# Scaling and transposing the rows of x by f32 matmuls with diagonal matrices instead of DMA transposes, with eight row buffers and one recurrence moved to VectorE

## The chip, the cores and the metric

One core of a Trainium2 chip runs the whole program. The metric is device time in microseconds (us), lower is better. The time before is the median of 3 runs.

## What is computed

Two blocks run one after the other on x, 2048 rows of 1024 values, all f32. Only the first part of the first block is touched:

```python
def first_block(x, norm_gain, w_in, ssm_a_re, ssm_a_im, ssm_log_dt, ...):
    h = rmsnorm(x, norm_gain) @ w_in          # 1024 -> 3072 columns
    # 512 columns u for the state-space mixer, 512 z, and 4 x 512 for a gated short convolution
    y_ssm = s5_mixer(u, a_re, a_im, log_dt, b_re, b_im, c_re, c_im, d, ...)
    y_conv = short_conv_mixer(...)
    # gates, w_out, residual, norm
```

`rmsnorm` divides each row by its root mean square and multiplies by the gain. `s5_mixer` makes its discrete parameters from `a_re`, `a_im` and `log_dt` (exponentials, sines, cosines, a division) and runs a complex linear recurrence along the rows. The second block (adaptive layer norm, a convolution module, a gated recurrence, chunked attention, a feed-forward part) is far larger, and no line of it is edited.

## The kernel before

TensorE (PE) works on f16. Each f32 operand is split into a high f16 part and a low f16 part that holds the rest, and each product is made of three f16 matmuls: high by low, low by high, high by high, the lines L417, L418 and L419 of the helper `mm3`. An activation split is made by `k.split`: the high part by ScalarE (ACT, L405), the low part by VectorE (DVE, L406). A scheduler (the Tile framework) fixes the order of the instructions on each engine at build time, from the order in which the program issues them and from the buffers they need. On the chip, each engine takes its own list strictly in order and waits where an operand is late.

`stage_in` is the stage that is edited. x is read in 16 tiles of 128 rows, into a ring of `NX` buffers. For each tile, `x1(t)` sums the squares of the rows (ACT, L410) and makes the reciprocal root by some ten very small DVE operations (L387 to L396). `x2(t)` then splits the scaled rows into hi and lo, and two DMA transposes, issued on the SP queue (L813, L814), put them into `xT`, four pairs of tiles with the 1024 columns on the partitions and 512 rows each. The rows in `xT` feed every product of the stage:

- `first(n)`, for n = 0 to 3, is done while the first four tiles and the first four weight blocks come in. It multiplies what has just become possible, in pieces of 128 rows: 24, 72, 120 and 168 matmuls, 384 in all. `first(n)` takes weight block n with the tiles before n, then tile n with the weight blocks 0 to n.
- `uproj(1)`, `uproj(2)` and `uproj(3)` do the other three groups of 512 rows: 96 matmuls of 512 columns each. `put_u` (ACT, L821) brings each result from PSUM into `u`.
- Then follow the other 20 weight blocks of w_in over all of `xT`, the long stream of 512-column matmuls that starts at 151 us in the profile. The text calls it the chunk stream.

The state-space parameters are a background task, `ssm_all`. From `t == 8` on the scheduler mixes its instructions into the loop. `ssm_params` reads `a_re`, `a_im` and `log_dt` (L473, L474, and L476 twice) and works on 128x16 values with more than 150 DVE operations, the first of which on `log_dt` is L445. `ssm_fb` then makes, for each of four groups `fb`, powers E and H by complex multiplications `cmul`, 48 tensor operations each, all on GpSimd (POOL, through `k.gtt`, L360); ACT copies H into wide tiles (L647, L648), and PE transposes E and multiplies (L628, L629, L637, L638).

The DMA that matters below reads one value per pair of groups and repeats it over 64 partitions:

```python
for g in range(2):
    nc.sync.dma_start(ldt[g * 64:(g + 1) * 64], a["ssm_log_dt"][0].rearrange("(r g) -> g r", g=2)[g].partition_broadcast(64))
```

Of the kernel before, what the change touches and what calls it, by code (L numbers as in the profile page):

```python
# [9 lines left out]
F32 = mybir.dt.float32  # L10
F16 = mybir.dt.float16
BF16 = mybir.dt.bfloat16
# [3 lines left out]
ALU = mybir.AluOpType  # L16
# [4 lines left out]
P = 128  # L21
T = 2048
D = 1024
KB = 8
# [2 lines left out]
RN = 1.5 * 2.0 ** 23  # L27
TWO_PI = 2.0 * math.pi
ALPHA = 2.0 ** 0.25
NX = 5  # L30


class Arena:
# [64 lines left out]
    def new(self, shape, dt=F32, name="t"):  # L98
        size = {F32: 4, I32: 4, F16: 2, BF16: 2, U8: 1}[dt]
        m = 1  # L100
        for d in shape[1:]:
            m *= d
        st, n = self.take(-(-m * size // 4))
        v = self.ap[:shape[0], st:st + n]
        if dt != F32:
            v = v.bitcast(dt)
        v = v[:, :m]
        if len(shape) > 2:
            names = ["d%d" % i for i in range(len(shape) - 1)]
            v = v.rearrange("p (%s) -> p %s" % (" ".join(names), " ".join(names)), **{nm: d for nm, d in zip(names[1:], shape[2:])})  # L110
        self.live[id(v)] = (v, st, n, name)
        return v
# [441 lines left out]
def ssm_fb(k, a, pm, fb, u_d, y_d):  # L554
    nc = k.nc
    gp = nc.gpsimd
    v = nc.vector
    NP = 4
    prs = slice(fb * 4, fb * 4 + 4)
    shp = [P, NP, 16]  # L560
    flat = lambda t: t.rearrange("p a b -> p (a b)")
    bc = lambda nm: pm[nm][:, prs].unsqueeze(2).to_broadcast(shp)
    new = lambda s, nm: k.new(s, F32, nm)
# [14 lines left out]
    Hr, Hi = new([P, NP, 8, 16], "Hr"), new([P, NP, 8, 16], "Hi")  # L578
    t1, t2 = new(shp, "cm1"), new(shp, "cm2")

    def cmul(orr, oi, xr, xi, yr, yi):
        k.gtt(t1, xi, yi, ALU.mult)
        k.gtt(orr, xr, yr, ALU.mult)
        k.gtt(orr, orr, t1, ALU.subtract)
        k.gtt(t2, xi, yr, ALU.mult)
        k.gtt(oi, xr, yi, ALU.mult)
        k.gtt(oi, oi, t2, ALU.add)

    cmul(Er[:, :, 0], Ei[:, :, 0], br, bi, bc("qr"), bc("qi"))
    k.free(br, bi)  # L590
    for j in range(7):
        cmul(Er[:, :, j + 1], Ei[:, :, j + 1], Er[:, :, j], Ei[:, :, j], bc("abr"), bc("abi"))
        if j == 3:
            yield
    yield
    C = []
    Cb = []
    for nm, c2 in zip(("ssm_c_re", "ssm_c_im"), cs2):
# [3 lines left out]
        pv = pt[:, :P].rearrange("p (r g h) -> p r g h", g=2, h=16)  # L602
# [4 lines left out]
        for g in range(2):  # L607
            sl = slice(g * 64, g * 64 + 64)
            nc.scalar.copy(c[sl], pv[sl, :, g])
            nc.scalar.mul(cb[sl, :, g], pv[sl, :, g], sgn)  # L610
        k.unbank(pt)
        C.append(c)
        Cb.append(cb)
    yield
    cmul(Hr[:, :, 0], Hi[:, :, 0], C[0], C[1], bc("abr"), bc("abi"))
    k.free(*C)
    for j in range(7):
        cmul(Hr[:, :, j + 1], Hi[:, :, j + 1], Hr[:, :, j], Hi[:, :, j], bc("abr"), bc("abi"))
        if j == 3:
            yield  # L620
    k.free(t1, t2)
# [23 lines left out]
    for g in range(2):  # L645
        sl = slice(g * 64, g * 64 + 64)
# [31 lines left out]
    for r in range(NP):  # L678
# [21 lines left out]
        t1, t2 = new([P, 256], "t1"), new([P, 256], "t2")  # L700
# [80 lines left out]
def stage_in(k, a, dr):  # L781
    nc = k.nc
    v = nc.vector
    gp = nc.gpsimd
    win = a["w_in"][0]
    inv_x = k.hold()
    gp.memset(inv_x, 1.0 / XS)
    xT = [k.pair([P, KB, TB], "xT%d" % tb) for tb in range(NTB)]
    gain = k.hold(KB)
    wu = Loader([Weight(k, win[:, f * P:(f + 1) * P], inv_x, rowmul=gain, mul=v.tensor_tensor if f < 3 else None) for f in range(4)])  # L790
    xs = {}

    ring = [k.new([P, D], F32, "x") for _ in range(NX)]

    def x0(t, after=None):
        xs[t] = ring[t % NX]
        if after is not None:
            v.tensor_copy(xs[t][:, 0:1], after)
        nc.sync.dma_start(xs[t], a["x"][0, t * P:(t + 1) * P, :])

    def x1(t):
        x = xs[t]
        hi, lo = k.pair([P, D], "xs")
        ss = k.sumsq(lo.bitcast(BF16), x)
        xs[t] = (x, hi, lo, k.rsqrt(ss, 1.0 / (D * XS * XS), 1e-6 / (XS * XS)))

    def x2(t):
        x, hi, lo, rs = xs.pop(t)
        k.split(hi, lo, x, rs)
        if t >= 16 - NX:  # L810
            k.free(x)
        sl = slice((t % 4) * P, (t % 4 + 1) * P)
        nc.sync.dma_start_transpose(out=xT[t // 4][0][:, :, sl], in_=hi)  # L813
        nc.sync.dma_start_transpose(out=xT[t // 4][1][:, :, sl], in_=lo)  # L814
        k.free(hi, lo)
        return lo[:, 0:1]

    u = [k.new([P, 8, 256], F32, "u") for _ in range(4)]

    def put_u(tb, fb, w, ps):  # L820
        nc.scalar.activation(u[fb][:, :, tb * 64:(tb + 1) * 64], ps.rearrange("p (c t) -> p t c", t=8), AF.Identity, scale=w.inv)  # L821
        k.unbank(ps)

    def uproj(tb):
        for fb in range(4):
            w = wu.get(fb)
            put_u(tb, fb, w, k.fm(w, xT[tb]))
            if tb == NTB - 1:
                w.free()
                nc.sync.dma_start(dr["u"][fb * P:(fb + 1) * P], u[fb])  # L830
                k.free(u[fb])
            k.bg.tick()

    def first(n):
        for t, f in [(t, n) for t in range(n)] + [(n, f) for f in range(n + 1)]:
            w = wu.ws[f]
            sl = slice(t * P, (t + 1) * P)
            k.mm3(ps0[f][:, sl], [(w.hi[:, kb], w.lo[:, kb]) for kb in range(KB)], [(xT[0][0][:, kb, sl], xT[0][1][:, kb, sl]) for kb in range(KB)])
        if n == 3:
            for f in range(4):  # L840
                put_u(0, f, wu.ws[f], ps0[f])

    x0(0)
    wu.ws[0].load()
    nc.sync.dma_start(gain, a["norm_gain"][0].rearrange("(k p) -> p k", p=P))
    for t in range(1, 4):
        x0(t)
    ps0 = [k.bank() for _ in range(4)]
    ssm = None
    for t in range(17):  # L850
        if 1 <= t <= 4:
            wu.ws[t - 1].split()
            x2(t - 1)
        if t == 4:
            for j in range(4, 8):
                x0(j)
        if t < 16:
            x1(t)
        if t < 4:
            if t:  # L860
                wu.ws[t].load()
            wu.ws[t].stat()
        if t > 4:
            x2(t - 1)
        if 1 <= t <= 4:
            first(t - 1)
        if t == 4:
            wu.n = [4, 4, 4]
        if 4 < t < 13:
            x0(t + 3)  # L870
        if t == 8:
            ssm = k.bg.add(ssm_all(k, a, dr), 1.0)
        if t == 10:
            uproj(1)
    uproj(2)
    uproj(3)
    cw = k.new([P, 4, 3], F32, "cw")
    for j in range(3):
        nc.sync.dma_start(cw[:, :, j], a["conv_w"][0, j].rearrange("(f p) -> p f", p=P))
    mod = k.bg.add(mod_rows(k, a, dr["mod"]), 0.8)  # L880
    cols = [c + fb * P for fb in range(4) for c in (2048, 1024, 1536, 2560)] + [512 + f * P for f in range(4)]
    chunks = Loader([Weight(k, win[:, c:c + P], inv_x, rowmul=gain) for c in cols])
    at = 0
    ssm[1] = SSM_RATE
    for fb in range(4):
        vv = k.new([P, 2 + T], F32, "vv")
        acc = k.new([P, T], F32, "acc")
        gp.memset(vv[:, 0:2], 0.0)
        for st in range(4):
            w = chunks.get(fb * 4 + st, 1)  # L890
            for tb in range(NTB):
                ps = k.fm(w, xT[tb])
                sl = vv[:, 2 + tb * TB:2 + (tb + 1) * TB]
                asl = acc[:, tb * TB:(tb + 1) * TB]
                if st == 0:
                    nc.scalar.activation(sl, ps, AF.Identity, scale=w.inv)
                elif st == 1:
                    v.scalar_tensor_tensor(sl, ps, w.inv, sl, op0=ALU.mult, op1=ALU.mult)
                    for j in range(3):
                        src = vv[:, j + tb * TB:j + (tb + 1) * TB]  # L900
                        if j == 0:
                            v.tensor_scalar(asl, src, cw[:, fb, 0:1], None, op0=ALU.mult)
                        else:
                            v.scalar_tensor_tensor(asl, src, cw[:, fb, j:j + 1], asl, op0=ALU.mult, op1=ALU.add)
                elif st == 2:
                    v.scalar_tensor_tensor(asl, ps, w.inv, asl, op0=ALU.mult, op1=ALU.mult)
                else:
                    zt = k.new([P, TB], F32, "zt")
                    nc.scalar.activation(zt, ps, AF.Silu, scale=w.inv)
                    v.tensor_tensor(asl, asl, zt, ALU.mult)  # L910
                    k.free(zt)
                k.unbank(ps)
                k.bg.tick()
            w.free()
            if st == 1:
                k.free(vv)
        nc.sync.dma_start(dr["yv"][fb * P:(fb + 1) * P], acc)
        k.free(acc)
    k.free(cw)
    return xT, chunks, ssm, mod  # L920
# [1349 lines left out]
XS = 1024.0  # L2270
# [84 lines left out]
```

## Time and profile before

| what | value |
|---|---|
| runs | 3268.93, 3275.31, 3273.25 us, median 3273.25 |
| profiled execution | 3276.22 us, span 3274.5, mean granted TensorE clock 0.967 |
| busy share | PE 93%, DVE 63%, ACT 34%, POOL 23% |
| first 151.5 us (stage up to the chunk stream) | PE busy 99.3 us (26.4 + 34.2 + 38.7 in three pieces) |
| the other 3123 us | PE busy 2948.9 us |

A row of the timeline reads: start, duration, engine, line, operation, output<-input, shape, and in brackets how long the engine had been idle before it and what ended that. Rows of a queue (SPq) are the issue of a DMA, not its transfer. Since PE is busy for nearly all of the later program, the first 151 us hold a good part of PE's idle time: 52 of 226 us.

### The profile page before, as it was taken

How to read it: one execution, taken by the hardware profiler on the slowest of the kernel's cores; microseconds unless marked ns; L12 is line 12 of the kernel's file. 1: busy time of each engine (PE TensorE's matmuls, PEld its weight loads, DVE VectorE, ACT ScalarE, POOL GpSimd, SP SyncE). 2: the span in 40 equal slices, each digit the busy share in tenths (PEclk: the TensorE clock that was granted, in tenths of full speed). 3: DMA queues.
4: the chain of work that ended last, by engine and by line, in shares of the span. 5: the costliest groups of instructions: out<-in, count | busy, mean ns of one | idle time of the engine just before them, and what ended most of it. 6: DMA issues, size and time to landing. Idle time of an engine off the chain costs nothing. (4 is left out here: it accounts for less than half of the span.)

```text
span 3274.5 us, 43302 instructions
## 1 busy us (share of the span) xinstructions
PE 3048.2 (93%) x16198; PEld 1532.2 (47%) x16198; DVE 2061.5 (63%) x4895; ACT 1116.8 (34%) x1745; POOL 760.0 (23%) x801
## 2 busy tenths in 40 slices
PE   6799999979799988999999878999999999899998
PEld 4344454534345654555555433444444444344443
DVE  5577887355864469999568877555555555543322
ACT  5322222584524565221333333444443333300000
POOL 0432533023332332110120223111111121023321
PEclk9899999989899998999999989999999999999999
DMA  8734443535773754100125798222331113723220
GB/s 181 166 92 111 121 125 80 120 100 152 215 219 74 138 117 106 39 14 33 62 78 140 170 250 216 90 78 78 102 110 54 58 52 119 244 68 113 68 73 31
DMA packets 549651, 364.57 MB, mean 111 GB/s; under 512 B 290152, under 2 KB 503592, under 8 KB 545344
## 3 DMA queue, kind: packets, MB, share of 16 engines
q1 hardware_dynamic: 549440, 361.81, 41.1%
q8 instruction: 127, 2.08, 0.3%
q14 instruction: 84, 0.69, 0.1%
HBM read 216.73 MB, written 84.70 MB: 92 GB/s over the span
## 5 line engine op out<-in xcount | busy, mean ns | idle before, releaser
L417 PE MATMUL psum<-arena 128*128 128x512 f16 (+2 forms) x4272 | 1601.9, 377 | 78.6 <-DMA arena<-arena 34.4
L418 PE MATMUL psum<-arena 128*128 128x512 f16 (+2 forms) x4272 | 1602.1, 376 | 8.2 <-DMA arena<-h_d 4.2
L419 PE MATMUL psum<-arena 128*128 128x512 f16 (+2 forms) x4272 | 1598.6, 376 | 0.2 <-DVE arena L406 0.2
L360 POOL TENSOR_TENSOR arena<-arena 128x64 f32<-128x64 f32 (+5 forms) x681 | 681.8, 1025 | 2089.2 <-DVE arena L2179 336.9
L417 PEld LDWEIGHTS <-arena 128*128 128x128 f16 x4272 | 426.0, 100 | 593.1 <-issue 101.1
L418 PEld LDWEIGHTS <-arena 128*128 128x128 f16 x4272 | 424.1, 99 | 492.1 <-issue 44.3
L419 PEld LDWEIGHTS <-arena 128*128 128x128 f16 x4272 | 424.2, 99 | 488.4 <-issue 26.1
L410 ACT ACTIVATE arena<-arena 128x1024 bf16<-128x1024 f32 (+2 forms) x218 | 237.7, 1091 | 487.0 <-DVE arena L2062 153.3
L406 DVE SCALAR_TENSOR_TENSOR arena<-arena,kept 128x1024 f16<-128x1024 f32 (+2 forms) x152 | 230.4, 1538 | 130.0 <-ACT arena L405 110.4
L2005 DVE TENSOR_TENSOR arena<-arena,psum 128x512 f32<-128x512 f32 x264 | 177.8, 684 | 206.0 <-PE psum L419 150.9
L405 ACT ACTIVATE arena<-arena,kept 128x1024 f16<-128x1024 f32 (+2 forms) x152 | 174.5, 1175 | 183.0 <-DVE kept L355 62.7
L406 DVE SCALAR_TENSOR_TENSOR arena<-arena,ring 128x1024 f16<-128x1024 f32 (+1 forms) x164 | 209.7, 1302 | 42.0 <-ACT arena L405 36.2
L405 ACT ACTIVATE arena<-arena,ring 128x1024 f16<-128x1024 f32 (+1 forms) x164 | 172.2, 1082 | 168.6 <-DVE ring L355 100.4
L1369 DVE SCALAR_TENSOR_TENSOR arena<-arena 128x512 f32<-128x512 f32 x240 | 177.9, 778 | 0.3
L1551 PE MATMUL psum<-arena 128*127 128x64 f32 (+6 forms) x896 | 106.2, 264 | 22.2 <-DVE arena L1554 21.1
L1551 PEld LDWEIGHTS psum<-arena 128*127 128x127 f32 (+6 forms) x896 | 102.0, 182 | 48.4 <-DVE arena L1554 29.8
L2179 DVE SCALAR_TENSOR_TENSOR arena<-psum,kept,arena 128x512 f32<-128x512 f32 x32 | 23.3, 747 | 144.0 <-PE psum L419 144.0
L770 DVE SCALAR_TENSOR_TENSOR arena<-arena 128x128 f32<-128x128 f32 x336 | 111.6, 367 | 1.8
L2051 ACT ACTIVATE arena<-arena,kept 128x1024 f32<-128x1024 f32 x44 | 49.8, 1142 | 124.1 <-DVE arena L2005 124.1
L1289 ACT ACTIVATE arena<-arena,ring,kept 128x640 f32<-128x640 f32 (+4 forms) x64 | 54.5, 851 | 81.8 <-DVE ring L1287 73.0
L373 PE MATMUL psum<-kept,ones 128*128 128x1 bf16 x82 | 13.3, 169 | 70.4 <-DVE kept L365 49.5
L1553 DVE TENSOR_TENSOR arena<-arena 128x256 f32<-128x256 f32 x112 | 54.9, 490 | 37.4 <-PE psum L1551 35.8
(318 smaller groups left out, 2583.2 us busy)
## 6 DMA issues: line engine op xcount, KB each, us to landing
arena<-in_w_in_dram SPq DMA_DIRECT2D x50, 512.0 KB
arena<-in_w_ada_dram SPq DMA_DIRECT2D x48, 512.0 KB
arena<-in_w_ffn_in_dram SPq DMA_DIRECT2D x44, 512.0 KB
arena<-in_w_ffn_out_dram SPq DMA_DIRECT2D x44, 512.0 KB
a_d<-arena SPq DMA_DIRECT2D x88, 256.0 KB
arena<-a_d SPq DMA_DIRECT2D x40, 512.0 KB
arena<-in_x_dram SPq DMA_DIRECT2D x32, 512.0 KB
x_d<-arena SPq DMA_DIRECT2D x32, 512.0 KB
```

What stands on the lines that cost most here:

```text
L360: self.nc.gpsimd.tensor_tensor(out, x, y, op)
L405: self.nc.scalar.activation(hi, src, AF.Identity, scale=s)
L406: self.nc.vector.scalar_tensor_tensor(lo, src, s, hi, op0=ALU.mult, op1=ALU.subtract)
L410: self.nc.scalar.activation(junk, src, AF.Square, accum_out=ss)
L417: self.nc.tensor.matmul(ps, lh, rh, start=start and i == 0, stop=False)
L418: self.nc.tensor.matmul(ps, lh, rl, start=False, stop=False)
L419: self.nc.tensor.matmul(ps, ll, rh, start=False, stop=stop and i == n - 1)
L770: v.scalar_tensor_tensor(ac, raw[:, kb], cc[:, kb:kb + 1], ac, op0=ALU.mult, op1=ALU.add)
L1369: v.scalar_tensor_tensor(acc[:, f], src, w, acc[:, f], op0=ALU.mult, op1=ALU.add)
L1551: nc.tensor.matmul(pv[:rows, bsl], KS[:, c * P:c * P + rows], q4[:, bsl], start=True, stop=True)
L1553: v.tensor_tensor(q4, q4, Fv[:, :, 0:1].to_broadcast([P, nb, hb]), ALU.mult)
L2005: v.tensor_tensor(out, x, ps, op)
```

## The change

- `NX` goes from 5 to 8, and the loads of x are issued in another place: the load of tile t + 3 in round t, from round 1 on.
- `x1` no longer makes room for hi and lo; it makes `dg`, the 128x128 identity times the reciprocal root of each row (DVE, L812).
- `x2` multiplies: for each of the 8 blocks of 128 columns, one f32 matmul with the block of x as the stationary operand and `dg` as the moving one (L819). That gives the block transposed and scaled, in two PSUM banks. ACT copies the banks into the hi half of `xT` (L826, 128x1024 from PSUM), and DVE subtracts hi from PSUM into the lo half (L827). The two DMA transposes go.
- The `ssm_all` task starts at `t == 7`, `uproj(1)` stands at `t == 9`, `uproj(2)` at `t == 13`.
- The H products of group `fb == 0` are made on DVE (L582 to L587).

```diff
-NX = 5
+NX = 8
...
     def x1(t):
         x = xs[t]
-        hi, lo = k.pair([P, D], "xs")
-        ss = k.sumsq(lo.bitcast(BF16), x)
-        xs[t] = (x, hi, lo, k.rsqrt(ss, 1.0 / (D * XS * XS), 1e-6 / (XS * XS)))
+        junk = k.new([P, D], BF16, "junk")
+        ss = k.sumsq(junk, x)
+        k.free(junk)
+        dg = k.new([P, P], F32, "dg")
+        v.tensor_scalar(dg, k.ident, k.rsqrt(ss, 1.0 / (D * XS * XS), 1e-6 / (XS * XS)), None, op0=ALU.mult)
+        xs[t] = (x, dg)
 
     def x2(t):
-        x, hi, lo, rs = xs.pop(t)
-        k.split(hi, lo, x, rs)
+        x, dg = xs.pop(t)
+        ps = k.bank(2)
+        for kb in range(KB):
+            nc.tensor.matmul(ps[:, kb * P:(kb + 1) * P], x[:, kb * P:(kb + 1) * P], dg, start=True, stop=True)
         if t >= 16 - NX:
             k.free(x)
+        k.free(dg)
+        pv = ps.rearrange("p (k t) -> p k t", t=P)
         sl = slice((t % 4) * P, (t % 4 + 1) * P)
-        nc.sync.dma_start_transpose(out=xT[t // 4][0][:, :, sl], in_=hi)
-        nc.sync.dma_start_transpose(out=xT[t // 4][1][:, :, sl], in_=lo)
-        k.free(hi, lo)
-        return lo[:, 0:1]
+        hi, lo = (xT[t // 4][x_][:, :, sl] for x_ in range(2))
+        nc.scalar.copy(hi, pv)
+        v.tensor_tensor(lo, pv, hi, ALU.subtract)
+        k.unbank(ps)
...
-        if 4 < t < 13:
+        if 0 < t < 13:
             x0(t + 3)
-        if t == 8:
+        if t == 7:
             ssm = k.bg.add(ssm_all(k, a, dr), 1.0)
-        if t == 10:
-            uproj(1)
-    uproj(2)
+        if t in (9, 13):
+            uproj(t // 4 - 1)
     uproj(3)
...
+    ht = v.tensor_tensor if fb == 0 else k.gtt
...
-    cmul(Hr[:, :, 0], Hi[:, :, 0], C[0], C[1], bc("abr"), bc("abi"))
+    cmul(Hr[:, :, 0], Hi[:, :, 0], C[0], C[1], bc("abr"), bc("abi"), ht)
```

The edit also moves instructions. Three places matter for what follows; the rows give the line, the operation, output<-input and the shape, and xN stands for N in a row.

The SP queue before, where the state-space parameters are issued; L799 loads a tile of x (here tiles 12 and 13), L813 and L814 are the transposes of earlier tiles:

```order
L799 DMA arena<-in_x_dram 128x1024
L813 DMA_TRANSPOSE arena<-arena 128x8x128
L814 DMA_TRANSPOSE arena<-arena 128x8x128
L799 DMA arena<-in_x_dram 128x1024
L474 DMA arena<-in_ssm_a_im_dram 128x16x1
L476 DMA arena<-in_ssm_log_dt_dram 64x16x1 x2
```

The SP queue after, from its beginning; L804 loads a tile of x, L169 a weight block:

```order
L804 DMA arena<-in_x_dram 128x1024
L169 DMA arena<-in_w_in_dram 128x8x128
L857 DMA kept<-in_norm_gain_dram 128x8x1
L804 DMA arena<-in_x_dram 128x1024 x3
L169 DMA arena<-in_w_in_dram 128x8x128
L804 DMA arena<-in_x_dram 128x1024
L169 DMA arena<-in_w_in_dram 128x8x128
L804 DMA arena<-in_x_dram 128x1024
L169 DMA arena<-in_w_in_dram 128x8x128
L804 DMA arena<-in_x_dram 128x1024 x4
L473 DMA arena<-in_ssm_a_re_dram 128x16x1
L474 DMA arena<-in_ssm_a_im_dram 128x16x1
```

The two loads of `log_dt` stand right behind these rows. They have moved ahead of the loads of x from tile 10 on, and nothing but the loads of tiles 0 to 9, four weight blocks, the gain, `a_re` and `a_im` is issued before them.

VectorE (DVE) before, around L445, the first operation that needs `log_dt`; L406 makes the lo half of a row tile, L538 to L540 work on `a_re` and `a_im`, L387 to L396 are the reciprocal roots:

```order
L406 SCALAR_TENSOR_TENSOR arena<-arena,ring 128x1024
L396 SCALAR_TENSOR_TENSOR ring<-ring 128x1
L392 SCALAR_TENSOR_TENSOR ring<-ring 128x1
L396 SCALAR_TENSOR_TENSOR ring<-ring 128x1
L538 TENSOR_TENSOR arena<-arena 128x16
L539 TENSOR_TENSOR arena<-arena 128x16
L540 RECIPROCAL arena<-arena 128x16
L387 TENSOR_SCALAR ring<-ring 128x1
L388 TENSOR_SCALAR ring<-ring 128x1
L389 TENSOR_SCALAR ring<-ring 128x1
L445 TENSOR_SCALAR arena<-arena 128x16
```

VectorE after, from L445 on; L812 makes a diagonal matrix, and L827 at the end is the lo half of row tile 2:

```order
L445 TENSOR_SCALAR arena<-arena 128x16
L396 SCALAR_TENSOR_TENSOR ring<-ring 128x1
L812 TENSOR_SCALAR arena<-ident,ring 128x128
L392 SCALAR_TENSOR_TENSOR ring<-ring 128x1
L387 TENSOR_SCALAR ring<-ring 128x1
L446 TENSOR_SCALAR arena<-arena 128x16
L396 SCALAR_TENSOR_TENSOR ring<-ring 128x1
L388 TENSOR_SCALAR ring<-ring 128x1
L447 TENSOR_SCALAR arena<-arena 128x16
L392 SCALAR_TENSOR_TENSOR ring<-ring 128x1
L389 TENSOR_SCALAR ring<-ring 128x1
L448 SCALAR_TENSOR_TENSOR arena<-arena 128x16
```

L827 of tile 2 stands three rows behind these. Before, L445 stood behind the splits of most of the row tiles; after, only the lo halves of tiles 0 and 1 stand ahead of it, and those of tiles 2 to 15 behind it. On PE, each tile's 8 f32 matmuls (16 instructions in the trace, since each f32 matmul is recorded as two) stand just ahead of the `first(t)` that uses the tile. For the later tiles they stand in blocks, 35 in a row (the last three of tile 4, and tiles 5 to 8) ahead of `uproj(1)`, 32 ahead of `uproj(2)` and 24 ahead of `uproj(3)`.

More of the change, by code (lines that the diff above doesn't have):

```diff
@@ L579, in ssm_fb, with cmul @@
     t1, t2 = new(shp, "cm1"), new(shp, "cm2")
[L581 to L587, printed above, removed]
+    def cmul(orr, oi, xr, xi, yr, yi, tt=k.gtt):
+        tt(t1, xi, yi, ALU.mult)
+        tt(orr, xr, yr, ALU.mult)
+        tt(orr, orr, t1, ALU.subtract)
+        tt(t2, xi, yr, ALU.mult)
+        tt(oi, xr, yi, ALU.mult)
+        tt(oi, oi, t2, ALU.add)
     cmul(Er[:, :, 0], Ei[:, :, 0], br, bi, bc("qr"), bc("qi"))
@@ L595, in ssm_fb @@
     yield
+    if fb == 0:
+        k.free(t1, t2)
     C = []
@@ L614, in ssm_fb @@
     yield
-    cmul(Hr[:, :, 0], Hi[:, :, 0], C[0], C[1], bc("abr"), bc("abi"))
+    ht = v.tensor_tensor if fb == 0 else k.gtt
+    if fb == 0:
+        t1, t2 = new(shp, "cm1"), new(shp, "cm2")
+    cmul(Hr[:, :, 0], Hi[:, :, 0], C[0], C[1], bc("abr"), bc("abi"), ht)
     k.free(*C)
     for j in range(7):
-        cmul(Hr[:, :, j + 1], Hi[:, :, j + 1], Hr[:, :, j], Hi[:, :, j], bc("abr"), bc("abi"))
+        cmul(Hr[:, :, j + 1], Hi[:, :, j + 1], Hr[:, :, j], Hi[:, :, j], bc("abr"), bc("abi"), ht)
         if j == 3:
@@ L853, in stage_in @@
             x2(t - 1)
-        if t == 4:
-            for j in range(4, 8):
-                x0(j)
         if t < 16:
```

## The prediction

> **What bounds the kernel now.** I read the page's first line, then windows of the trace, because a mean over stages with different limits says nothing about one of them.
>
> ```profile
> PE 3048.2 (93%) x16198; PEld 1532.2 (47%) x16198; DVE 2061.5 (63%) x4895; ACT 1116.8 (34%) x1745; POOL 760.0 (23%) x801
> 0.00:50.00 50.00, 26.36 (x388) 25.61 (x388) 35.06 (x128) 30.47 (x43) 4.60 (x14) 0.97 1.02 236
> 50.00:100.00 50.00, 34.17 (x133) 14.20 (x134) 24.34 (x147) 19.67 (x28) 0.14 (x2) 0.76 0.71 134
> 100.00:151.50 51.50, 38.73 (x185) 19.96 (x184) 21.11 (x88) 21.04 (x42) 36.92 (x103) 0.88 0.59 138
> 151.50:667.00 515.50, 507.23 (x2429) 248.69 (x2428) 354.12 (x952) 158.04 (x279) 152.46 (x332) 0.99 0.45 111
> 667.00:3274.50 2607.50, 2441.67 (x13067) 1223.74 (x13064) 1626.85 (x3583) 887.55 (x1358) 565.88 (x351) 0.97 0.39 108
> ```
>
> A window row gives its bounds and length, then busy time of PE, PE's weight loads, DVE, ACT and POOL, then the granted clock, the DMA share and GB/s. PE bounds the program: 507 of 515 us in the stream behind the edited stage, 2442 of 2608 behind that. The edited stage is the first 151.5 us, where PE works 99.3 us and is idle 52.2. So PE work added there costs its full length, and an edit gains only by removing PE's gaps. The timeline of PE shows them, in brackets:
>
> ```profile
> 15.61 0.27 PE L417 MATMUL psum<-arena 128*128 128x128 f16 x1 [6.02 <-DMA arena<-arena]
> 24.85 0.27 PE L417 MATMUL psum<-arena 128*128 128x128 f16 x2 [2.21 <-DMA arena<-arena]
> 26.69 0.27 PE L418 MATMUL psum<-arena 128*128 128x128 f16 x1 [1.56 <-DMA arena<-arena]
> 50.84 0.58 PE L417 MATMUL psum<-arena 128*128 128x512 f16 x1 [4.03 <-DMA arena<-arena]
> 89.44 0.58 PE L417 MATMUL psum<-arena 128*128 128x512 f16 x1 [14.58 <-DMA arena<-arena]
> 147.35 0.47 PE L628 MATMUL psum<-ident,arena 128*128 128x128 f32 x1 [12.77 <-ACT arena L821]
> 151.11 0.61 PE L417 MATMUL psum<-arena 128*128 128x512 f16 x1
> 151.51 0.63 PE L418 MATMUL psum<-arena 128*128 128x512 f16 x1
> 155.78 0.39 PE L418 MATMUL psum<-arena 128*128 128x512 f16 x1
> 156.01 0.38 PE L419 MATMUL psum<-arena 128*128 128x512 f16 x1
> ```
>
> The first five gaps end with the landing of a DMA transpose. The sixth ends when ACT gets to `put_u`. The chunk stream starts at 151.1; until 155.8 its matmuls go at 0.43 us each and then at 0.22. So a gap of some us also costs the 4.7 us of slow start behind it, about 2.3 us of lost work. Why 14.58 us at 89.44? The SP queue and DVE tell:
>
> ```profile
> 59.59 3.66 SPq L476 DMA_DIRECT2D arena<-in_ssm_log_dt_dram  x2
> 63.35 11.53 SPq L813 DMA_TRANSPOSE arena<-arena  x1
> 82.96 0.58 SPq L799 DMA_DIRECT2D arena<-in_x_dram  x1
> 64.57 0.15 DVE L389 TENSOR_SCALAR ring<-ring 128x1 int32<-128x1 int32 x1
> 83.01 0.17 DVE L445 TENSOR_SCALAR arena<-arena 128x16 f32<-128x16 f32 x1 [18.29 <-DMA arena<-in_ssm_log_dt_dram]
> 84.56 1.28 DVE L406 SCALAR_TENSOR_TENSOR arena<-arena,ring 128x1024 f16<-128x1024 f32 x1
> 64.00:80.00 16.00, 10.86 (x51) 4.71 (x49) 0.60 (x5) 1.55 (x2) 0.00 (x0) 0.92 0.05 0
> ```
>
> The two loads of `log_dt` are issued at 59.59 and have landed at 83.0, 23.4 us later. In the window 64 to 80 the DMA share is 0.05, less than one engine of sixteen, and about 0 GB/s move: a trickle of tiny packets through which the transposes issued at 63.35 have to wait, and in which DVE stands at L445 for 18.3 us. This is how I explain the 14.58 us. [...]
>
> **The change, part by part.**
>
> ```profile
> 168.96 1.95 PE L656 MATMUL psum<-arena 128*128 128x128 f32 x16
> 170.74 0.38 PE L417 MATMUL psum<-arena 128*128 128x512 f16 x1
> L656 PE MATMUL psum<-arena 128*128 128x128 f32 x64 | 7.9, 276 | 0.2 <-DVE arena L643 0.2
> L821 ACT ACTIVATE arena<-psum,kept 128x512 f32<-128x512 f32 x16 | 10.6, 676 | 0.1
> L2005 DVE TENSOR_TENSOR arena<-arena,psum 128x512 f32<-128x512 f32 x264 | 177.8, 684 | 206.0 <-PE psum L419 150.9
> L768 DVE TENSOR_SCALAR arena<-arena 128x128 f32<-128x128 f32 x48 | 16.6, 358 | 6.2 <-DMA arena<-in_w_ada_dram 6.2
> ```
>
> 1. *The f32 matmuls, on PE's path: +28.4 us.* Sixteen records of L656, the same shape, take 170.74 - 168.96 = 1.78 us, 0.111 each; two records make one matmul. 16 tiles by 8 matmuls by 0.222 are 28.4 us. The other end is busy time, 7.9 us for 32 matmuls, 31.6 for 128; I take the pitch, since neighbours overlap.
>
> 2. *The transposes go: -22.4 us of gaps at 24.85, 26.69, 50.84 and 89.44.* Without transposes no PE wait ends with DMA packets behind the trickle. The gap of 6.02 at 15.61 is exchanged for about the same: diagonal matrix, eight slow matmuls, ACT copy and DVE subtraction. Each of these reads 128x1024 from PSUM, twice the 0.676 (L821) and 0.684 us (L2005) above, so 1.35 and 1.37 us. My walk puts the first product of `first(0)` at 16.6 instead of 15.6.
>
> 3. *The log_dt wait moves into a worse place: +16 us.* On SP the two loads now stand behind tile 9, whose buffer comes free when tile 1 has been multiplied, at about 22 us in my walk; they are issued at about 24. With the 23.4 us of before they land at 47.4; a backlog of loads could add some us, so 46 to 52, and I take 48.5. On DVE, L445 stands ahead of the lo halves of tiles 2 to 15 (before, behind twelve splits). So DVE stops at about 28, with everything behind it queued, and with it the `first(2)` of PE. PE by then has done `first(0)`, `first(1)`, the f32 matmuls of tiles 0 to 2 and the 48 matmuls of weight block 2 with tiles 0 and 1, until about 35. It goes on when DVE has done L445, 13 small operations (0.17 us each, L445) and L827, at 51. The wait is 51 - 35 = 16 us. If the loads landed ahead of 32, it would be nothing; that is the lower bound.
>
> 4. *New gaps: +13 us.* (a) 3.0 between tile 0's f32 matmuls and `first(0)`, and 2.7 for tile 1: PE waits for copy and subtraction, with nothing else in its list. Term 2 has the first 3.0 already, so 2.7 count. (b) 1.5 for tile 3, whose lo half stands behind 60 small parameter operations. (c) 3.5 ahead of `uproj(1)`: tiles 4 to 8 are 40 f32 matmuls, 8.9 us, but the pairs of PSUM banks are few, and ACT has four `put_u` (0.676 each) and two table loads ahead of the copies.
>
> ```profile
> 122.63 1.28 ACT L747 ACT_TABLE_LOAD   x1
> 144.82 0.62 ACT L647 COPY arena<-arena 64x512 f32<-64x512 f32 x1 [11.88 <-POOL arena L360]
> L360 POOL TENSOR_TENSOR arena<-arena 128x64 f32<-128x64 f32 x384 | 137.8, 395 | 84.9 <-ACT arena L609 46.1 <-ACT arena L690 15.2 <-DVE arena L406 12.1
> ```
>
> A table load is 1.28 us. (d) 2.5 ahead of `uproj(3)`, for the copy and subtraction of tile 15. Then 1.0 for the first product (16.6 against 15.6) and 2 for the slow start after the long gap, moved to 51, where 128-column matmuls run: 2.7 + 1.5 + 3.5 + 2.5 + 1.0 + 2 = 13.2. Bounds 5 (copies hidden, no bank wait) and 25 (1 us more for each of twelve tiles).
>
> 5. *H on DVE: -12.8 us and its slow start, -2.3.* Before, ACT stands 11.88 us at L647 for POOL's H, `put_u` queues behind it, and PE behind `put_u`: 12.77 at 147.35. The 48 operations of 128x64 took POOL 0.395 us each, 19 us. On DVE they cost between L445's 0.17 (128x16) and L768's 0.358 (128x128), 8 to 17 us; nearest is 0.2, 10 us. They stand right behind the lo half of tile 15 (about 144) and end about 154, inside `uproj(3)`, 96 matmuls by 0.216 or 20.7 us. If that cover went, PE would wait at L635's copies for at most the 10 us.
>
> 6. *NX = 8, dg, the freed splits: 0.* Loads run ahead by three tiles; in the stage no gap ends with a load of x. The 16 dg are 16 by 0.358 or 5.7 us on a DVE that also loses 16 splits (1.28 each) for 16 subtractions (1.37).
>
> Sum: 28.4 - 22.4 + 16 + 13.2 - 12.8 - 2.3 = +20. One thing goes back:
>
> ```profile
> 17.29 0.31 PE L417 MATMUL psum<-arena 128*128 128x128 f16 x1
> 17.40 0.31 PE L418 MATMUL psum<-arena 128*128 128x128 f16 x1
> 29.57 0.22 PE L417 MATMUL psum<-arena 128*128 128x128 f16 x1
> 29.63 0.22 PE L418 MATMUL psum<-arena 128*128 128x128 f16 x1
> ```
>
> Before, the 128-column matmuls run slowly (0.107 us apart) in 17 to 29 us, about a hundred of them, and then at 0.056. The f32 matmuls now keep PE at work from 10 us on, so I let 80 of the hundred run fast: 80 by 0.051, -4. That makes +16, the chunk stream at 167 to 168 instead of 151.1. Behind it PE is 98% busy, so the shift goes through to the end. The profiled execution, 3276.22 us (span 3274.5), would be 3292; it lies 3.0 above the median, so 3289 against 3273.25. Later stages come out in another order with the same work; I give them 0 with bounds of 8 each way.
>
> A rule of the clock: the 4.7 us above are the row. The Trainium skill, page "TensorE: Matmul & The Clock Gate", section "Part 1: The HAM clock gate", says that the clock opens after some 3.4 us of sustained work and that this varies from run to run. By it, each slow start would cost 1.7 instead of 2.3 us, and the sum would be under 1 us higher.
>
> **The rivals.**
>
> *Faster (0.20).* `log_dt` doesn't hold DVE. The point that decides is whether both loads have landed before DVE reaches L445 with PE still in work, before about 32 us. For it: the queue is emptier without 32 transposes, and the 23.4 us of before were partly queueing. Against it: during 64 to 80 nothing else moved, so 16 of the 23.4 are the trickle itself. Without the 16 us and its slow start, and with (c) and (b) at half, the sum is 16 - 16 - 2 - 3 = -5; with bounds from term 4 to -13. Time 3260 to 3268, centre 3265.
>
> *No change (0.17).* The wait is there, but half of it is hidden: issued at 18 rather than 24, landing at 42, PE stands 7 to 9 us and the new gaps are at their lower end: 16 - 8 - 7 = +1, 3274.
>
> *Worse (0.23).* The two-bank pairs and ACT's list make each of twelve tiles wait 1 to 1.5 us more, since a copy and a subtraction of 1.35 us each are longer than the 1.78 us of the eight matmuls: 16 + 15 = +31, 3304.
>
> *The H edit does nothing.* H on DVE starts late, as it stands behind every lo half, and the gap of 12.77 returns in part: half of 15 is 7 more, 3297; it lies inside the range, and I give it no chance apart.
>
> **How the numbers follow.** My forecast holds 0.40, at 3289, with 3280 to 3299 for itself. About 0.2% (6.5 us) is what a measurement of this kernel can tell from no change, so the faster rival splits: its centre is beyond 3266.7 only for the larger part of the bounds, and I put 0.18 on faster; same gets 0.18; slower 0.64. The range leaves out the lower half of the faster rival and the upper part of the worse one: 3262 to 3306.
>
> **What would show it.** DVE's L445 should start near 48 us, after a wait of about 20 us on `log_dt`, and PE should stand 12 to 18 us ahead of the f16 matmuls of tile 2. L819 should be busy 28 to 32 us. The chunk stream should start at 163 to 172. No L633 or L635 wait of over 3 us should stand ahead of it. I am wrong if L445 starts before 35 us, if the pairs of banks show gaps of over 1.5 us per tile, or if stages behind 667 us change their idle time by more than 8 us.

## The result: 3329.6 us, slower, and most of it far behind the edit

The changed kernel takes 3329.64 us (median of 4 runs, 3326.79 to 3331.98) against 3274.28 us before. The ratio is 1.0171, with a 95% interval of 1.0153 to 1.0188: 56 us slower. The prediction had 3289 in a range of 3262 to 3306. The sign was right, the size was not, and most of the 56 us has a cause that the prediction had at nothing.

The page's first line of the changed kernel, and then windows of both traces, cut at places where the same work has been done (the start of the chunk stream, the end of that stream, and the 4584th and the 6384th of the f16 products of `mm3`). The columns are bounds and length, busy time of PE, PE's weight loads, DVE, ACT and POOL, then the granted clock, DMA share and GB/s. First before:

```profile
0.00:151.10 151.10, 98.86 (x704) 59.62 (x705) 80.12 (x360) 70.78 (x109) 41.67 (x118) 0.87 0.77 169
151.10:667.00 515.90, 507.63 (x2430) 248.83 (x2431) 354.52 (x953) 158.44 (x280) 152.46 (x332) 0.99 0.45 111
667.00:1173.10 506.10, 445.96 (x2864) 235.88 (x2862) 304.49 (x766) 251.01 (x346) 170.06 (x130) 0.94 0.57 148
1173.10:1812.20 639.10, 587.28 (x3676) 348.37 (x3674) 527.30 (x1390) 229.81 (x471) 106.19 (x58) 0.95 0.27 73
1812.20:3274.50 1462.30, 1408.42 (x6532) 639.49 (x6529) 795.05 (x1428) 406.73 (x542) 289.63 (x164) 0.98 0.37 110
```

Then the changed kernel:

```profile
PE 3093.2 (93%) x16454; PEld 1571.7 (47%) x16454; DVE 2072.0 (62%) x4959; ACT 1116.4 (34%) x1744; POOL 734.4 (22%) x753
0.00:163.80 163.80, 126.20 (x959) 89.02 (x959) 86.81 (x422) 67.18 (x108) 26.16 (x70) 0.92 0.38 110
163.80:680.00 516.20, 506.80 (x2435) 249.18 (x2435) 362.28 (x956) 160.29 (x278) 151.41 (x339) 0.99 0.45 110
680.00:1188.80 508.80, 450.82 (x2860) 237.10 (x2860) 299.61 (x764) 253.02 (x348) 166.50 (x123) 0.93 0.56 147
1188.80:1868.10 679.30, 599.35 (x3676) 356.59 (x3674) 528.45 (x1389) 227.43 (x469) 112.77 (x59) 0.92 0.25 67
1868.10:3330.30 1462.20, 1410.07 (x6532) 639.82 (x6529) 794.87 (x1430) 408.47 (x544) 277.59 (x163) 0.98 0.38 110
```

Take the lengths pair by pair: the edited stage is 12.7 us longer, the next two stretches 0.3 and 2.7, the fourth 40.2, and the last is the same within 0.1. The fourth is the attention and the recurrence of the second block. No line of it is edited, and the records on every engine are as many as before to within 2. Its 40 us are 28 us more of idle PE (679.30 - 599.35 = 79.95 against 51.82) and 12 us more of busy PE for the same 3676 records, at a granted clock of 0.92 instead of 0.95.

In the edited stage the trace reads almost as forecast. PE's gaps, DVE's wait and the f32 matmuls:

```profile
10.34 3.60 PE L819 MATMUL psum<-arena 128*128 128x128 f32 x16 [0.55 <-DVE kept L355]
15.04 0.22 PE L417 MATMUL psum<-arena 128*128 128x128 f16 x1 [1.10 <-ACT arena L826]
16.30 0.22 PE L418 MATMUL psum<-arena 128*128 128x128 f16 x1 [1.04 <-DVE arena L827]
50.06 0.26 PE L418 MATMUL psum<-arena 128*128 128x128 f16 x1 [15.95 <-DVE arena L827]
79.92 0.38 PE L417 MATMUL psum<-arena 128*128 128x512 f16 x1 [3.19 <-ACT arena L826]
162.21 0.41 PE L642 MATMUL psum<-arena 128*128 128x32 f32 x2 [2.45 <-DVE ring L354]
164.22 0.61 PE L417 MATMUL psum<-arena 128*128 128x512 f16 x1
24.50 2.06 SPq L476 DMA_DIRECT2D arena<-in_ssm_log_dt_dram  x2
47.49 0.17 DVE L445 TENSOR_SCALAR arena<-arena 128x16 f32<-128x16 f32 x1 [16.45 <-DMA arena<-in_ssm_log_dt_dram]
48.79 1.22 DVE L827 TENSOR_TENSOR arena<-psum,arena 128x1024 f16<-128x1024 f32 x1
L819 PE MATMUL psum<-arena 128*128 128x128 f32 x256 | 32.9, 291 | 0.6 <-DVE kept L355 0.6
```

`log_dt` is issued at 24.50 and has landed at 47.49. DVE stands 16.45 us at L445, and PE 15.95 us for the lo half of tile 2 behind it. The chunk stream starts at 164.2 instead of 151.1.

### The profile page after: what moved, and what is told of

Its sections match the earlier page's. It is cut to its first block, busy times and chain, and to the rows that moved or that the text cites. A ratio compares the mean times of both kernels' runs of the same rounds, so it can differ in the third digit from the quotient of the medians.

```text
span 3330.3 us, 43783 instructions
## 1 busy us (share of the span) xinstructions
PE 3093.2 (93%) x16454; PEld 1571.7 (47%) x16454; DVE 2072.0 (62%) x4959; ACT 1116.4 (34%) x1744; POOL 734.4 (22%) x753
## 5 line engine op out<-in xcount | busy, mean ns | idle before, releaser
L360 POOL TENSOR_TENSOR arena<-arena 128x64 f32<-128x64 f32 (+4 forms) x633 | 656.3, 1060 | 2141.0 <-DVE arena L2187 340.3
L406 DVE SCALAR_TENSOR_TENSOR arena<-arena,kept 128x1024 f16<-128x1024 f32 (+2 forms) x152 | 224.2, 1496 | 116.5 <-ACT arena L405 102.9
L406 DVE SCALAR_TENSOR_TENSOR arena<-arena,ring 128x1024 f16<-128x1024 f32 (+1 forms) x148 | 180.3, 1267 | 18.5 <-ACT arena L405 18.1
L405 ACT ACTIVATE arena<-arena,ring 128x1024 f16<-128x1024 f32 (+1 forms) x148 | 150.9, 1073 | 58.9 <-DVE ring L355 26.3
L1559 PE MATMUL psum<-arena 128*96 128x64 f32 (+6 forms) x896 | 107.6, 267 | 24.8 <-DVE arena L1562 24.6
L1559 PEld LDWEIGHTS psum<-arena 128*96 128x96 f32 (+6 forms) x896 | 103.8, 185 | 51.8 <-DVE arena L1562 24.4
```

Of the source, the lines that this page charges most:

```text
L360: self.nc.gpsimd.tensor_tensor(out, x, y, op)
L405: self.nc.scalar.activation(hi, src, AF.Identity, scale=s)
L406: self.nc.vector.scalar_tensor_tensor(lo, src, s, hi, op0=ALU.mult, op1=ALU.subtract)
L1559: nc.tensor.matmul(pv[:rows, bsl], KS[:, c * P:c * P + rows], q4[:, bsl], start=True, stop=True)
```

## The experiments

Why would an unedited stage get slower? The program takes its buffers from one arena of memory. A request takes a free piece that is large enough, by preference one that has been free for long and is tight; where none fits, the helper `retry` lets the background tasks take one step, which may free something, and asks again. So the pieces that the edited stage leaves free decide, far behind, when a request succeeds, and with that where a load stands in the program. In the attention stage the load of the first row group for the recurrence (`load_hT`, two DMAs from `h_d`) needs two pieces of 2048 words, and is asked for while only one free piece is that large, though much of the arena's 50800 words is free (18576 of them in the kernel before, 12432 in the changed one). In the building of the kernel before, this request failed twice, in the changed one five times. The traces show when the load is issued, first before and then after:

```profile
1223.58 0.92 SPq L1121 DMA_DIRECT2D arena<-h_d  x2
```

```profile
1272.67 4.18 SPq L1129 DMA_DIRECT2D arena<-h_d  x2
```

From the start of their stretch that is 50.5 us before and 83.9 us after. In between PE has only work of the attention stage, which waits for the transposes of the softmax. The rows of the list of waits for them (total, times, longest), 1173 to 1287 us before, then 1188 to 1323 us after, where the lines stand 8 lower:

```profile
PE psum L1321 <- DMA arena<-arena: 2.8, 2, 2.4
PE psum L1323 <- DMA arena<-arena: 2.5, 5, 0.9
```

```profile
PE psum L1329 <- DMA arena<-arena: 15.1, 7, 4.1
PE psum L1331 <- DMA arena<-arena: 5.7, 7, 2.4
```

These are 15.5 us more, in the first piece of the stretch, up to the 4884th product:

```profile
1173.09:1286.98 113.89, 94.64 (x858) 54.62 (x856) 93.52 (x228) 72.62 (x114) 31.25 (x21) 0.90 0.60 134
```

```profile
1188.77:1322.37 133.60, 99.10 (x862) 59.00 (x860) 108.47 (x267) 78.36 (x123) 34.17 (x22) 0.80 0.54 113
```

So this piece has 19.7 of the 40 us, and the waits account for most of it. Most of the rest comes behind the load, once PE works on the recurrence: 7.9 us up to the 5184th product, 8.2 more up to the 5784th. What PE loses there is not traced further.

**Theory A:** the buffers that the edited stage leaves behind cost the 40 us. **Rival B:** the new work itself costs them, by the clock or the DMA traffic.

All the runs below were timed beside runs of the kernel before on their own chip, and these differ (medians of before: 3265.67 for the first four, 3271.96 for the next four, 3267.09 for the last two). So the ratio is what counts; it is not the quotient of these medians, and microseconds given beside it are its distance from 1, times 3274.

### Stage after, places of before

The arena gets a table of offsets for all buffers up to the first tile behind the stage (`Hz`), and there its list of free pieces is set to what it was before. The three further x buffers, the diagonal matrices and the junk tiles lie in places that are free at their time. From `Hz` on, buffers, issue order and, on PE, the order of all but the first of the matmuls are those of the kernel before.

```diff
+PLAN = {'x': [16384, 17408, 18432, 19456, 20480, ...], 'u': [21504, ...], ...}
+SB_AT = ([(16384, 21504, 39), (21504, 23552, 70), ...], 85)
...
-        st, n = self.take(-(-m * size // 4))
+        st, n = self.take(-(-m * size // 4), self.plan[name].pop(0) if self.plan.get(name) else None)
...
+    if fb == 0:
...
+        (k.sb.segs, k.sb.now), (k.ps.segs, k.ps.now) = (list(SB_AT[0]), SB_AT[1]), (list(PS_AT[0]), PS_AT[1])
+        k.sb.plan = {}
     Hz = new([P, NP, 2, 2, P], "Hz")
```

> The changed stage, with the buffers placed by a table where the kernel before places them, up to the first tile behind the stage; from there the program is issued and ordered as before. Theory A (the stage itself costs 12 us by the two traces, and the other 42 us come because the changed buffers of the stage leave the free memory cut differently, which delays loads and reorders the attention stage): 3274 + 12 = 3286 us, between 3280 and 3292. Rival B (the 42 us come from the new work itself, for instance a slower clock after more f32 matmuls or from DMA traffic that has moved): 3320 to 3330.

Measured: 3280.21 us, ratio 1.0039 (1.0028 to 1.0050), 13 us. The stretch that was 639.10 before and 679.30 in the changed kernel is now

```profile
1186.00:1819.40 633.40, 580.40 (x3676) 345.65 (x3675) 527.68 (x1391) 229.53 (x471) 105.72 (x58) 0.97 0.28 73
```

Theory A holds, and B falls: all the new work is in this kernel, and the 40 us are gone. The chunk stream starts at 167.2 us here, 16 us later than before.

### Stage before, places of after

The same table method the other way round: the kernel before, with its arena brought to the state that the changed kernel leaves at `Hz`. The buffers that both have get the offsets of the changed kernel; the hi and lo row tiles lie in places that are free at their time.

```diff
+PLAN = {...}
+SB_AT = ([(16384, 22528, 64), (22528, 23552, 67), ...], 90)
...
```

> The stage as before, with the buffers placed where the changed kernel places them at its end; from there the program is issued and ordered as in the changed kernel. Theory A: 3274 + 42 = 3316 us, between 3308 and 3324. Rival B: 3274, within 6.

Measured: 3316.72 us, ratio 1.0147 (1.0132 to 1.0162), 48 us, without one f32 matmul in the stage. The stretch:

```profile
1176.70:1850.60 673.90, 595.30 (x3677) 354.86 (x3675) 528.59 (x1388) 226.30 (x467) 106.24 (x59) 0.92 0.25 67
```

So the two parts add up, within their intervals: stage 1.0039, places 1.0147; together they would make 1.019, and the change has 1.0171 (1.0153 to 1.0188).

### The load alone, late

The kernel before, where nothing but the load is put later in the program (what follows is then placed and ordered in other ways too, since the arena goes on from there).

```diff
         if nh is None and tb + 1 == NTB:
+            for _ in range(5):
+                k.bg.tick()
             nh = load_hT(k, dr["h1"], 0)
```

> The kernel before, with five steps of the background work put ahead of the request for the buffers of the first row group of the recurrence stage, so that this load is issued late, as it is in the changed kernel after five failed requests for memory. Theory A1 (what costs is that the load comes late and the TensorE has only attention work until then): 20 to 60 us slower, 3294 to 3334, most of it lost between 1170 and 1400 us. Rival A2 (what costs is which buffers share memory, not when the load is issued): 3274, within 10.

Measured: 3304.68 us, ratio 1.0110 (1.0095 to 1.0126), 36 us. In its building the request still fails four times behind the five steps, so nine steps stand ahead of the load; it is issued 82.0 us into its stretch, about as late as in the changed kernel. A weaker dose, three steps, behind which the request does not fail:

> As the kernel with the late load, but three steps of background work ahead of the request instead of five; since they free the memory, no request fails there, and the load stands one step later than in the kernel before instead of five. Theory A1 (the delay of the load sets the loss): 3 to 12 us slower than before, ratio 1.001 to 1.004. Rival A2 (any other order of buffers behind it costs as much): ratio 1.009 to 1.013 again.

Measured: 3283.38 us, ratio 1.0046 (1.0032 to 1.0061), 15 us. That lies between the two expectations, a little above A1's upper end.

### Five row buffers in the changed kernel

```diff
-NX = 8
+NX = 5
```

> The changed kernel with one number changed: five row buffers instead of eight, buffers placed freely. The build then has one failed request for memory in the attention stage, against five in the changed kernel and three in the kernel before, so the load of the first row group of the recurrence stage should be issued early. Theory A: ratio to the kernel before 1.002 to 1.008 (the stage's 13 to 16 us, and less than 12 us behind it). Rival (a long row ring has nothing to do with it, the later stages are slow with any changed stage): 1.014 to 1.019.

Measured: 3310.63 us, ratio 1.0125 (1.0110 to 1.0140). It lies between the two expectations, so theory A in this form missed, and its rival too: I had gone by the failed requests for this load, one against five. The load is issued 61.4 us into its stretch all the same (at 1246.69). The right measure is not how often a request fails, but when the load is issued. The windows of the three kernels (late load, three steps, five buffers), one row each:

```profile
1174.35:1843.49 669.14, 589.70 (x3677) 353.02 (x3674) 529.88 (x1386) 228.49 (x473) 100.14 (x58) 0.93 0.26 69
```

```profile
1175.29:1824.09 648.80, 587.84 (x3677) 350.63 (x3675) 523.46 (x1387) 225.82 (x469) 106.42 (x59) 0.94 0.27 70
```

```profile
1185.30:1843.48 658.18, 588.07 (x3676) 351.39 (x3674) 530.57 (x1389) 229.06 (x472) 112.49 (x59) 0.95 0.26 70
```

| kernel | load issued, us into the stretch | length of the stretch, us |
|---|---|---|
| stage after, places of before | 49.4 | 633.4 |
| before | 50.5 | 639.1 |
| after, five buffers | 61.4 | 658.2 |
| before, three steps | 62.7 | 648.8 |
| before, late load | 82.0 | 669.1 |
| stage before, places of after | 83.2 | 673.9 |
| after | 83.9 | 679.3 |

The length goes with the time of the load, to about 10 us. Each length is from one execution, and the whole program differs by some 13 us between executions of one kernel (3259.57 to 3272.35 us for the kernel before on the first chip), so a few us between two rows mean nothing. What makes the other 10 (five buffers against three steps, at the same time of the load) is open: these kernels differ in everything that is placed behind the load. That the placement costs the time is shown by crossing the stages; that it does so through the time of this load is shown only as far as these seven rows go together.

### log_dt loaded in long rows

The first kernel (stage after, places of before), with the load of `log_dt` as 128 rows of 32 values, from which two small DVE copies pick:

```diff
-    for g in range(2):
-        nc.sync.dma_start(ldt[g * 64:(g + 1) * 64], a["ssm_log_dt"][0].rearrange("(r g) -> g r", g=2)[g].partition_broadcast(64))
+    l32 = tp.tile([P, 32], F32, tag="l32", name="l32")
+    nc.sync.dma_start(l32, a["ssm_log_dt"][0].partition_broadcast(P))
+    for g in range(2):
+        v.tensor_copy(ldt[g * 64:(g + 1) * 64], l32.rearrange("p (r g) -> p g r", g=2)[g * 64:(g + 1) * 64, g])
```

> As the first of these (changed stage, places of before), but log_dt is loaded as 128 rows of 32 values and picked apart by two small VectorE copies, instead of 2048 single values. If the wait for log_dt costs what the trace says (16 us of TensorE and a slow start): 3286 - 17 = 3269 us, between 3264 and 3276; L445 starts before 35 us and the gap of 16 us at 34 us is under 4. Rival (something else on VectorE holds the lo half of tile 2 then): 3280 to 3288.

Measured: 3262.62 us, ratio 0.9987 (0.9977 to 0.9996), 17 us below the kernel without this edit on the same chip, and a little under the range expected. The gap ahead of tile 2, 15.95 in the changed kernel, is in the kernel without this edit

```profile
51.68 0.27 PE L503 MATMUL psum<-arena 128*128 128x128 f16 x1 [18.18 <-DVE arena L917]
```

and with it

```profile
34.33 0.22 PE L504 MATMUL psum<-arena 128*128 128x128 f16 x1 [1.30 <-DVE arena L920]
30.91 0.15 DVE L564 COPY arena<-arena 64x16 f32<-64x16 f32 x1
```

with no wait ahead of the copy, the first operation on `log_dt`. So term 3 of the prediction, the wait, is worth what its row says. The same edit in the kernel before, where nothing else is changed and a table of the same kind holds the buffers behind the stage in their places:

> The kernel before, with one edit: log_dt loaded as 128 rows of 32 values; buffers and order behind the stage as before. If the 14.58 us gap of TensorE at 89 us comes from the log_dt packets that the transposes wait behind, it goes with its slow start: 3266 - 17 = 3249 us, between 3246 and 3256. Rival (the transposes are late for another reason, and the gap stays): 3262 to 3268.

Measured: 3248.08 us, ratio 0.9937 (0.9916 to 0.9959), 21 us. The transposes behind the load are now issued without standing, 1.24 instead of 11.53 us, and PE's gap of 14.58 is gone:

```profile
60.08 2.88 SPq L562 DMA_DIRECT2D arena<-in_ssm_log_dt_dram  x1
63.06 1.24 SPq L906 DMA_TRANSPOSE arena<-arena  x1
64.39 1.27 SPq L907 DMA_TRANSPOSE arena<-arena  x1
```

### H on VectorE, alone

The kernel before, with only the H products of `fb == 0` on DVE, and the places behind the stage held:

```diff
...
-    cmul(Hr[:, :, 0], Hi[:, :, 0], C[0], C[1], bc("abr"), bc("abi"))
+    ht = v.tensor_tensor if fb == 0 else k.gtt
+    cmul(Hr[:, :, 0], Hi[:, :, 0], C[0], C[1], bc("abr"), bc("abi"), ht)
...
```

> The kernel before, with one edit: the H products of the first group on VectorE instead of GpSimd; buffers as before. If the 12.77 us gap at 147 us comes from these products on GpSimd: 3266 - 15 = 3251 us, between 3247 and 3256. Rival (VectorE gets to them late, or another wait takes the place): 3260 to 3268.

Measured: 3262.97 us, ratio 0.9982 (0.9970 to 0.9994), 6 us and not 15. The rival holds: the wait on POOL's H is gone, but PE stands 10.4 us a few instructions further, for a PSUM bank that a small DVE operation (L439 here, L354 in the kernel before) has to read. A row of the waits, 120 to 150 us:

```profile
PE psum L728 <- DVE ring L439: 10.4, 1, 10.4
```

The last of the H products, the small operation and the matmul that waits for it:

```profile
139.16 0.23 DVE L672 TENSOR_TENSOR arena<-arena 128x64 f32<-128x64 f32 x1
144.88 0.21 DVE L439 TENSOR_SCALAR ring<-psum 128x1 int32<-128x1 int32 x2
145.08 0.64 PE L728 MATMUL psum<-arena 128*128 128x32 f32 x2 [10.42 <-DVE ring L439]
```

The small operation stands in DVE's list behind the H products, and behind work on `w_ada`. So of PE's 10.4 us, which begin at 134.66, the first 4.7 are again a wait for the H products, now on DVE.

In the changed stage, with the short `log_dt` load and the places of before, H went back to GpSimd:

> The changed stage with the short log_dt load and the places of before, as measured at 0.9987 of the time before, but with H of the first group back on GpSimd. If H on VectorE is worth its gap here too: 3262.6 + 15 = 3277 us, between 3272 and 3282, and a gap of about 12 us ahead of the matmuls of L633 or L642. Rival (in the changed stage the products start earlier and GpSimd hides them): 3262 to 3266.

Measured: 3274.09 us, ratio 1.0005 (0.9994 to 1.0016). Against 0.9987 for the same stage with H on DVE that is 0.18%, 6 us, with an interval of about 1 to 11 us; the two were measured on different chips. The 3274.09 us lie in the range of the first expectation, but that range was reckoned from a time on the other chip. By the traces the chunk stream starts 11.4 us later, behind two gaps of 4.3 and 6.1 us instead of one of 12. So H on DVE is worth less than 15 in this stage too, but how much is not settled.

### Both edits in the kernel before

> The kernel before with both edits, the short log_dt load and H of the first group on VectorE, and the DMA transposes kept. If the two gaps are independent: 3266 - 30 = 3236 us, between 3230 and 3244. Rival (they overlap, since with log_dt early the products come earlier too): 3245 to 3252. Against the changed stage with the short load (3262.6) this gives the price of the f32 matmuls in place of the transposes: 26 us, 28 expected from their own time.

Measured: 3242.37 us, ratio 0.9915 (0.9899 to 0.9930), 28 us faster than before. It has the lowest ratio of all, though its interval overlaps that of the short load alone. It keeps the DMA transposes. With f32 matmuls the stage has 0.9987, measured on another chip: 0.72%, 24 us, is what they cost here in place of the transposes, together with the gaps that go and come with them, the eight row buffers, the other positions of `uproj` and the earlier parameter task.

## Why the prediction was wrong

Its terms, with what was measured:

1. *f32 matmuls, +28.4.* The trace has 32.9 us busy for the 256 records, somewhat more than forecast, above all since those of tile 0 run slowly (16 records in 3.60 us). The 24 us between whole kernels hold parts of terms 2 and 4 too, so they do not measure this term alone. About right.
2. *Transpose gaps, -22.4.* Gone in the trace; no gap ends with a transpose in the changed stage. That the 14.58 of it came from the load of `log_dt`, as forecast, the short load in the kernel before shows. Right.
3. *The log_dt wait moved, +16.* Measured 15.95, from 34.1 to 50.1 (forecast 35 to 51), L445 at 47.49 (forecast 48.5); taking it away, in the kernel with the places of before, gives 17 us. Right.
4. *New gaps, 13.2.* Ahead of tile 0's products PE waits 1.10 and 1.04 (forecast 3.0), and the first of them comes at 15.04 (forecast 16.6). PE waits, ahead of `uproj(1)`, 3.19 (forecast 3.5). The 2.45 at 162.21 stand behind `uproj(3)` and end with a small DVE operation, not ahead of it as forecast. About right in size, not in every place.
5. *H on DVE, -15.* The gap of 12.77 is not there in the changed kernel, but the edit alone gives 6 us in the kernel before: too large. The 48 operations were put at 10 us. In the changed kernel they take 8.3, from 138.81 to 147.09, so their time was not the error. The first two and the last of them on DVE:

```profile
138.81 0.22 DVE L582 TENSOR_TENSOR arena<-arena 128x64 f32<-128x64 f32 x1
138.94 0.22 DVE L583 TENSOR_TENSOR arena<-arena 128x64 f32<-128x64 f32 x1
146.88 0.21 DVE L587 TENSOR_TENSOR arena<-arena 128x64 f32<-128x64 f32 x1
```

   What was missed is that on DVE the products stand ahead of a small operation that PE needs for a bank: the step of naming "what is late next" was answered too kindly there.
6. *The sum for the stage, +16.* With the later part undisturbed (places of before), the chunk stream starts 16 us later and the kernel takes 1.0039, 13 us. In the changed kernel itself it starts 13.1 us later. Of the -4 in it only a part came, since between 24 and 28 us the f16 matmuls again follow at 0.107 us. About right.

The step that failed is the sentence behind the sum: "Later stages come out in another order with the same work; I give them 0 with bounds of 8 each way." The work is the same, but the order isn't free: the fourth stretch lost 40 us. I had seen that the order of the instructions differs almost to the end of the program, and priced this by nothing. The row that should have warned is the share of the stretch: DVE is busy for 527.30 of 639.10 us there and PE for 587.28, so neither has much spare time to make up a delay, and a load that comes 33 us late leaves PE with the work that waits on transposes. None of the rivals named it: the one that came nearest in time, 3304, had gaps at the pairs of banks for its cause, and these are not in the trace. But the last sign of being wrong named it, and it came: behind 667 us (680 in the changed kernel) PE is idle for 190 us instead of 166. "Slower" came true by another cause for three quarters of its size, which is luck.

## What to carry to other kernels

Where buffers come from one allocator and a failed request moves work, an edit of an early stage changes the stages behind it, even with no line of them touched; compare order and buffers there first, and give a reshuffled stage a bound of the order of its idle time, not a few microseconds (in this one case 40 us were lost where PE had 52 idle). To measure such an edit by itself, hold the rest still: force the places and the free list behind the stage, and cross both stages with both placements. And a wait that shows on one engine may have its cause in another's queue: the transposes looked like the thing to remove, and the load of single values ahead of them was.

## What was not expected of the hardware

By the row of the short load, a DMA of 128 rows of 32 values is issued in 2.88 us and the next transpose in 1.24, where the two loads of the same 32 values as single elements took 23.4 us to land and held the next transpose's issue for 11.53 us. In the window 64 to 80 us of the kernel before, 1716 packets moved, 0.01 MB in all. The Trainium skill, page "DMA: Bandwidth & Descriptors", section "Rules for kernel authors", asks for an outermost dimension whose size is a multiple of 16, ideally the 128 partitions, so that all 16 engines take part. The short load has 128 there and the loads of single elements have 64, so this rule does not tell them apart, and a DMA share of 0.05 can be one engine at work or sixteen that mostly wait. That the form of the load makes the difference is shown; by which mechanism is not. And DVE operations of 128x64 f32 start 0.13 us apart (138.81 and 138.94 above) although each is recorded with 0.22 us, so recorded durations of small operations must not be added up.
